# Neighbourhood attention: one biased pass over a unit's own and context scores, one exponential per unit

## The chip, the cores and the metric

The kernel runs on one core of a Trainium2 chip. The metric is the device time of one execution in microseconds (us); lower is better. The kernel before took 2827.46 us as the median of 3 runs (2826.29 to 2831.8).

## The reference

Two layers work on 1024 latent tokens (a grid of 16 rows by 64 columns, 1024 features) and 256 context tokens. Each layer projects the tokens, mixes them in four head groups A to D, projects the result, and then routes tokens through 16 experts. The change is in group A, 2-D neighbourhood attention with 4 heads of 64 features. A query attends to the 8 x 16 latent keys around it, with a learned bias by offset, and, without bias, to all 256 context keys; one softmax runs over both:

```python
s_win = (einsum('bqhd,brqjhd->bhqrj', q_row, k_win) * scale + bias).reshape(B, H, GRID_W, nw)
s_ctx = einsum('bqhd,blhd->bhql', q_row, kc) * scale
p = softmax(concatenate([s_win, s_ctx], axis=-1), axis=-1)
out = einsum('bhqrj,brqjhd->bqhd', p_win, v_win) + einsum('bhql,blhd->bqhd', p_ctx, vc)
```

## The kernel before

**Units.** `mixers` (L2047) makes a list of units and hands it to `pipeline` (L722). In group A a unit is 128 queries (two grid rows) of one head: 8 units to a head, 32 to a layer, numbered here 0 to 31. A head's units 0, 1, 6 and 7 are outer ones: they score 8 rows of keys (512 columns). Units 2 to 5 are inner ones (9 rows, 576 columns). In layer 0 four context units run ahead of group A; after it, in both layers, come the units of group D. Two units that follow each other (`q` 0 and 1) are a pair and share the tiles `pth` and `ptl`, the sums and the output `oA`.

**A unit's steps.** `scores` (L849): PE multiplies queries with keys into two PSUM tiles `SA`, the first with 256 or 320 columns, the second with 256 columns of own keys and 256 of the context. The DVE pass `window` (L858; on the chip one CUSTOM instruction and one that reads its accumulator) adds the bias table `tt`, keeps the maximum and writes to the SBUF tile `P` (PA in the trace). Own columns go through it in two passes; the context's 256 have only their maximum taken (L872). L874 takes the maximum over the three: `nmA`, negated. `exps` (L877): ACT takes the exponential of the context part out of PSUM (L883), then of the own part within `P` (L886), each with its sum. In an inner unit POOL sets a pad of 64 columns in `P` to 0 (L882). `turn` (L889): PE transposes 128-column chunks of `P` into PSUM tiles `pT`, up to four chunks to a tile, ACT copies each to `pth` (L104, rounded), and DVE writes the rest to `ptl` (L105): first the 2 context chunks, then 4, then (inner) 1. `values` (L903): PE multiplies them with the values into `oA`; ACT copies that to `oT` (L699), PE turns it back into `oP`, and ACT scales it by the reciprocal of the summed sums (`inv_sums`, L702) into `oh` (L717).

**Order.** On PE, DVE and ACT the order of instructions is the order in which `pipeline` writes them; each engine runs its list in order. Stage s interleaves, in rounds, the scores of unit s + 1, the exponentials of unit s and the turn of unit s - 1: a round runs each of the three up to its next `yield`. After the rounds comes one step of side work and then `values` and `finish` of earlier units. `oT` is written in even stages; the first half of a pair's products with the values, and `oP` and `oh` of the pair before, in odd ones. Side work of prep_d (L1050), a tile `hT4` (PE transposes, an ACT copy, a DVE rest) per stage, lies in stages 15 to 22 of both layers and 28 to 31 of layer 0. POOL's list is made by a scheduler.

**Buffers.** PSUM tiles `SA` take 4 banks (`m1`); `pT`, `hT4`, `oA` and `oP` share 4 more (`b1`, L94), a new tile taking the one that has been given back longest.

```python
                todo = []
                if s + 1 < n:
                    todo.append(units[s + 1].scores())
                if 0 <= s < n:
                    todo.append(units[s].exps())
                if 1 <= s <= n:
                    todo.append(units[s - 1].turn())
```

Of the kernel before, what the change touches and what calls it, by code (L numbers as in the profile page):

```python
# [13 lines left out]
AF = mybir.ActivationFunctionType  # L14
ALU = mybir.AluOpType
AX = mybir.AxisListType
# [15 lines left out]
NEG = -1e30  # L32
# [15 lines left out]
def f32(ap):  # L48
    return ap.bitcast(F32)
# [27 lines left out]
class Kernel:  # L77
# [730 lines left out]

    def bias_tables(self, i, h):

        nc, a = self.nc, self.a
        raw = self.half([128, 16, 64], name="tabr")
        nc.gpsimd.memset(raw, 0.0)
        pad = a["na_pad"]
        src = bass.AP(tensor=pad.tensor, offset=pad.offset + (i * H + h) * 15 * 128, ap=[[1, 64], [128, 15], [1, 64]])

        nc.sync.dma_start(raw[0:64, 0:15], src)
        nc.sync.dma_start(raw[64:128, 1:16], src)
        for _ in range(4):
            yield  # L820
        tt = self.wpage([128, 23, 64], name="tt")
        m = self.cmask[:, None, :].to_broadcast([128, 14, 64])
        nc.gpsimd.tensor_tensor(tt[:, 0:14], raw[:, 1:15, ::-1], m, ALU.add)
        nc.gpsimd.tensor_copy(tt[:, 14:23], tt[:, 2:11])
        nc.gpsimd.memset(tt[64:128, 14], NEG)
        nc.gpsimd.memset(tt[0:64, 22], NEG)
        self.tabs[h] = tt
        yield

    def units_a(self, i, out):  # L830
        nc, k = self.nc, self

        class Unit:
            delays = ()

            def __init__(u, h, g, q, first):
                u.h, u.g, u.q = h, g, q
                u.first = first or u
                u.inner = g in (1, 2)
                u.r = 4 * g + 2 * q  # L840
                u.k0 = min(max(u.r - 4, 0), 8)
                u.nk = 9 if u.inner else 8
                u.w = u.nk * 64
                u.n = 5 if u.inner else 4
                u.c_lo = (0, 0, 2, 4)[g]

            def scores(u):
                q = k.qA[u.h][:, u.r * 64:u.r * 64 + 128]

                w, k0 = u.w - 256, u.k0 * 64  # L850
                u.S = k.m1([128, 512], name="SA"), k.m1([128, 512], name="SA")
                k_h, tt = k.kA[u.h], k.tabs[u.h]
                u.P = k.half([128, 6 * 128 + 256], name="PA")
                mx = k.small([128, 3], name="mxA")
                s0 = 14 if u.inner else u.k0 - u.r + 6
                bias = tt[:, s0:s0 + u.nk].rearrange("p s k -> p (s k)")

                def window(j, S, c):  # L858
                    nc.vector.tensor_tensor_reduce(out=u.P[:, c], in0=S, in1=bias[:, c], op0=ALU.add, op1=ALU.max,
                                                   scale=1.0, scalar=-3e38, accum_out=mx[:, j:j + 1])  # L860

                def dot(S, keys):
                    k.mm(S, q, keys[0], True, False)
                    k.mm(S, q, keys[1], False, True)

                dot(u.S[0][:, :w], [x[:, k0:k0 + w] for x in k_h])
                window(0, u.S[0][:, :w], slice(0, w))
                yield
                dot(u.S[1][:, :256], [x[:, k0 + w:k0 + w + 256] for x in k_h])
                dot(u.S[1][:, 256:], k.kAc[u.h])  # L870
                window(1, u.S[1][:, :256], slice(w, w + 256))
                nc.vector.tensor_reduce(mx[:, 2:3], u.S[1][:, 256:], axis=AX.X, op=ALU.max)  # L872
                u.nm = k.small([128, 1], name="nmA")
                nc.vector.tensor_reduce(u.nm, mx, axis=AX.X, op=ALU.max, negate=True)  # L874
                yield

            def exps(u):  # L877
                if u.q == 0:
                    u.sums = k.small([128, 2, 2], name="smA")
                w, P, sm = u.w, u.P, u.first.sums[:, u.q]  # L880
                if u.inner:
                    nc.gpsimd.memset(P[:, w:w + 64], 0.0)  # L882
                nc.scalar.activation(P[:, u.n * 128:u.n * 128 + 256], u.S[1][:, 256:], AF.Exp, bias=u.nm,  # L883
                                     accum_out=sm[:, 1:2])
                yield
                nc.scalar.activation(P[:, :w], P[:, :w], AF.Exp, bias=u.nm, accum_out=sm[:, 0:1])  # L886
                yield

            def turn(u):  # L889
                if u.q == 0:  # L890
                    u.pth, u.ptl = k.wpage([128, 8, 256], F32R, name="pth"), k.wpage([128, 8, 256], F32R, name="ptl")

                c0 = u.k0 // 2 - u.c_lo
                qq = slice(u.q * 128, (u.q + 1) * 128)
                pth, ptl = u.first.pth, u.first.ptl
                if u.inner:
                    z = 5 if u.q == 0 else 0
                    nc.gpsimd.memset(f32(pth[:, z, qq]), 0.0)
                    nc.gpsimd.memset(f32(ptl[:, z, qq]), 0.0)
                yield from k.pt_steps(pth[:, 6:8, qq], ptl[:, 6:8, qq], u.P[:, u.n * 128:], 2)  # L900
                yield from k.pt_steps(pth[:, c0:c0 + u.n, qq], ptl[:, c0:c0 + u.n, qq], u.P, u.n)

            def values(u, part):  # L903
                ch = [(c, k.vA[(u.c_lo + c) // 2][:, (u.c_lo + c) % 2, u.h]) for c in range(6 if u.inner else 4)]
                ch += [(6 + c, k.vA[4][:, c, u.h]) for c in range(2)]
                n = len(ch) // 2
                if part == 0:
                    u.o2 = k.b1([128, 256], name="oA")
                    u.rs = k.inv_sums(u.sums)
                for j in range(part * n, part * n + n):  # L910
                    c, v = ch[j]
                    k.pv1(u.o2, v, u.pth[:, c], u.ptl[:, c], j == 0, j == len(ch) - 1)
                if part:
                    u.oT = k.heads_T(u.o2)

            def after(u, step):
                if u.q == 0 and step in (3, 4):
                    u.values(step - 3)
                if u.q == 0 and step == 5:
                    u.finish()  # L920

            def finish(u):
                k.put_heads(u.oT, u.rs, lambda q: out(u.h, 2 * u.g + q), lambda: u.done(u.h, 2 * u.g + 1))

        units = []
        for h in range(H):
            for g in range(4):
                for q in range(2):
                    units.append(Unit(h, g, q, units[-1] if q else None))
        return units  # L930
# [1292 lines left out]
```

## Time and profile before

| what | us |
|---|---|
| median of 3 runs | 2827.46 |
| the profiled execution | 2829.49 |
| its span, first to last instruction | 2827.7 |
| PE busy in the span | 2684.8 (95%) |
| DVE busy | 2088.3 (74%) |
| ACT busy | 1710.8 (61%) |
| POOL busy | 339.6 (12%) |
| group A, layer 0, 329.5 to 422.8 | 93.3 |
| group A, layer 1, 1822.0 to 1909.5 | 87.5 |

The busy shares of the whole span are means over stages that have little in common. Group A is 6% of the span, so it has to be read by itself: by the busy time in its own two stretches, and by the rows of its own instructions. Matmuls are pipelined and overlap in the trace, so that a PE shown as busy may still be waiting a little between them.

### The profile page before, as it was taken

How to read it: one execution, taken by the hardware profiler on the slowest of the kernel's cores; microseconds unless marked ns; L12 is line 12 of the kernel's file. 1: busy time of each engine (PE TensorE's matmuls, PEld its weight loads, DVE VectorE, ACT ScalarE, POOL GpSimd, SP SyncE). 2: the span in 40 equal slices, each digit the busy share in tenths (PEclk: the TensorE clock that was granted, in tenths of full speed). 3: DMA queues.
4: the chain of work that ended last, by engine and by line, in shares of the span. 5: the costliest groups of instructions: out<-in, count | busy, mean ns of one | idle time of the engine just before them, and what ended most of it. 6: DMA issues, size and time to landing. Idle time of an engine off the chain costs nothing. (4 is left out here: it accounts for less than half of the span.)

```text
span 2827.7 us, 46563 instructions
## 1 busy us (share of the span) xinstructions
PE 2684.8 (95%) x17078; PEld 2129.7 (75%) x17078; DVE 2088.3 (74%) x4377; ACT 1710.8 (61%) x3319; POOL 339.6 (12%) x418
## 2 busy tenths in 40 slices
PE   7999899999899999999999999999999699999995
PEld 5788788887577777777765788788876588888874
DVE  5624687867887777777765842698868998999996
ACT  5522697965455555555544641597963577777774
POOL 0000120211111110101111001120211000010011
PEclk9999999999999999999999999999999799999998
DMA  7652311144978888888899555111154799999996
GB/s 306 211 149 63 78 34 49 61 150 173 325 266 286 285 289 285 302 287 291 294 342 340 166 198 149 42 42 49 57 174 163 282 368 359 380 388 385 384 378 243
DMA packets 234572, 641.37 MB, mean 227 GB/s; under 512 B 35654, under 2 KB 90566, under 8 KB 234344
## 3 DMA queue, kind: packets, MB, share of 16 engines
q1 hardware_dynamic: 212264, 590.61, 56.9%
q0 software_dynamic: 21936, 47.72, 6.9%
q8 instruction: 135, 2.21, 0.3%
q14 instruction: 93, 0.76, 0.1%
q10 hardware_dynamic: 144, 0.07, 0.0%
HBM read 576.80 MB, written 61.54 MB: 226 GB/s over the span
## 5 line engine op out<-in xcount | busy, mean ns | idle before, releaser
L104 ACT ACTIVATE ewh<-ewr 128x1024 fp32r<-128x1024 f32 x768 | 772.9, 1055 | 425.5 <-DMA ewr<-exp_w_up 145.4
L105 DVE TENSOR_TENSOR ewl<-ewr,ewh 128x1024 fp32r<-128x1024 f32 x768 | 894.0, 1218 | 152.7 <-ACT ewh L104 150.8
L111 PE MATMUL moeP<-ewh,xs 128*128 128x512 f32 x2048 | 665.5, 400 | 3.6 <-DVE xs L105 3.4
L111 PEld LDWEIGHTS moeP<-ewh,xs 128*128 128x128 f32 x2048 | 385.9, 189 | 102.7 <-issue 10.5
L111 PE MATMUL moeP<-ewl,xs 128*128 128x512 f32 x1024 | 407.4, 398 | 0.0
L111 PE MATMUL moeP<-ewh,ehs 128*128 128x512 f32 x1024 | 331.3, 397 | 1.3 <-DVE ehs L105 1.3
L111 PEld LDWEIGHTS moeP<-ewh,ehs 128*128 128x128 f32 x1024 | 192.2, 188 | 56.4 <-issue 10.3
L111 PEld LDWEIGHTS moeP<-ewl,xs 128*128 128x128 f32 x1024 | 194.0, 189 | 43.9 <-issue 2.3
L111 PE MATMUL mixp<-woh,cT 128*128 128x512 f32 x576 | 205.1, 410 | 0.0
L111 PE MATMUL moeP<-ewl,ehs 128*128 128x512 f32 x512 | 201.7, 394 | 0.1
L1606 PE MATMUL cx<-ewr,cxo 128*32 128x256 f32 x3072 | 189.3, 382 | 0.8 <-DVE cxo L1835 0.8
L105 DVE TENSOR_TENSOR ptl<-pT,pth 128x512 fp32r<-128x512 f32 (+2 forms) x288 | 164.3, 580 | 19.6 <-ACT pth L104 18.8
L120 PE MATMUL pT<-ident,PA 128*128 128x128 f32 x928 | 146.0, 275 | 8.3 <-ACT oh L717 3.7
L1606 PEld LDWEIGHTS cx<-ewr,cxo 128*32 128x32 f32 x3072 | 90.9, 110 | 82.8 <-issue 30.3
L104 ACT ACTIVATE pth<-pT 128x512 fp32r<-128x512 f32 (+2 forms) x288 | 149.5, 536 | 4.3 <-PE pT L120 1.3
L1106 DVE TENSOR_REDUCE mxA<-SD 128x1 f32<-128x512 f32 (+1 forms) x192 | 114.5, 597 | 38.4 <-PE SD L111 37.5
L120 PEld LDWEIGHTS pT<-ident,PA 128*128 128x128 f32 x928 | 112.7, 141 | 32.4 <-ACT oh L717 5.8
L111 PEld LDWEIGHTS mixp<-woh,cT 128*128 128x128 f32 x576 | 108.3, 188 | 24.9 <-issue 3.8
L111 PE MATMUL SD<-kT,qT 96*128 96x512 f32 x384 | 119.8, 420 | 5.8 <-ACT PA L1120 5.4
L111 PE MATMUL mixp<-wol,cT 128*128 128x512 f32 x288 | 113.4, 394 | 0.0
L111 PEld LDWEIGHTS moeP<-ewl,ehs 128*128 128x128 f32 x512 | 96.3, 188 | 22.3 <-DVE ewl L105 1.0
L1565 POOL DMA_INDIRECT xg<-hrow,tkii x32 | 55.8, 1743 | 416.4 <-PE tkp L111 95.2
(425 smaller groups left out, 5143.5 us busy)
## 6 DMA issues: line engine op xcount, KB each, us to landing
ewr<-exp_w_gate SPq DMA_DIRECT2D x132, 1024.0 KB
ewr<-exp_w_up SPq DMA_DIRECT2D x132, 1024.0 KB
ewr<-exp_w_down SPq DMA_DIRECT2D x132, 1024.0 KB
ada_w<-ada_w SPq DMA_DIRECT2D x96, 512.0 KB
qkv<-qkvr SPq DMA_DIRECT2D x18, 512.0 KB
xacc<-xm SPq DMA_DIRECT2D x18, 512.0 KB
hrow<-xm SPq DMA_DIRECT2D x18, 512.0 KB
fr<-w_in SPq DMA_DIRECT2D x16, 512.0 KB
```

Of the source, the lines that this page charges most:

```text
L104: self.nc.scalar.activation(hi, src, AF.Copy)
L105: self.parted = (lo_on or self.nc.vector).tensor_tensor(lo, src, f32(hi), ALU.subtract)
L111: self.nc.tensor.matmul(out, l, r, start=start, stop=stop)
L120: self.nc.tensor.transpose(out, src, self.ident[:p, :p])
L1106: nc.vector.tensor_reduce(mx[:, j:j + 1], u.S[j], axis=AX.X, op=ALU.max)
L1565: nc.gpsimd.indirect_dma_start(out=xg, out_offset=None, in_=self.hrow[0], in_offset=bass.IndirectOffsetOnAxis(ap=idl, axis=0))
L1606: nc.tensor.matmul(pc[32 * j:32 * j + 32, :], xc[:, k % 2, k // 2], raw[:, j * 256:(j + 1) * 256], start=(k == 0), stop=(k == KT - 1), til ...
```

## The change

- The bias table gets 4 more rows of 64 columns, set to 0 by POOL. The second pass of `window` runs over all 512 columns of the second `SA` tile at once: 256 own ones with their bias, 256 of the context with the zeros, written to two ranges of `P` (`ranges`). The separate maximum over the context falls away.
- One exponential within `P` over 768 (outer) or 896 columns (inner, the pad included) takes the place of two. The pad is set to -1e30 ahead of it, in `scores`, and no longer to 0 in `exps`. One sum per unit is left, so the addition of sums (L704) falls away.
- `turn` begins with the first 4 chunks. Where the own chunks end at place 6 (units 3 and 5 of a head) the 5 + 2 chunks are turned as 4 and 3; otherwise own chunks (4, or 4 and 1) come first and the context's 2 last.
- `exps` has one `yield` in place of two.

```diff
-        tt = self.wpage([128, 23, 64], name="tt")
+        tt = self.wpage([128, 27, 64], name="tt")
+        nc.gpsimd.memset(tt[:, 23:27], 0.0)
...
+    def ranges(self, x, c0, step):
+
+        x = x[:, c0:c0 + 256]
+        return bass.AP(tensor=x.tensor, offset=x.offset, ap=[x.ap[0], [step, 2], [1, 256]])
...
-                mx = k.small([128, 3], name="mxA")
+                if u.inner:
+                    nc.gpsimd.memset(P[:, u.w:u.w + 64], NEG)
+                mx = k.small([128, 2], name="mxA")
...
-                window(1, u.S[1][:, :256], slice(w, w + 256))
-                nc.vector.tensor_reduce(mx[:, 2:3], u.S[1][:, 256:], axis=AX.X, op=ALU.max)
+                window(1, u.S[1].rearrange("p (a k) -> p a k", a=2), k.ranges(P, w, gap),
+                       k.ranges(bias, b1, 23 * 64 - b1))
...
-                if u.inner:
-                    nc.gpsimd.memset(P[:, w:w + 64], 0.0)
-                nc.scalar.activation(P[:, u.n * 128:u.n * 128 + 256], u.S[1][:, 256:], AF.Exp, bias=u.nm,
-                                     accum_out=sm[:, 1:2])
-                yield
-                nc.scalar.activation(P[:, :w], P[:, :w], AF.Exp, bias=u.nm, accum_out=sm[:, 0:1])
+                P = u.P[:, :u.n * 128 + 256]
+                nc.scalar.activation(P, P, AF.Exp, bias=u.nm, accum_out=u.first.sums[:, u.q:u.q + 1])
                 yield
...
-                yield from k.pt_steps(pth[:, 6:8, qq], ptl[:, 6:8, qq], u.P[:, u.n * 128:], 2)
-                yield from k.pt_steps(pth[:, c0:c0 + u.n, qq], ptl[:, c0:c0 + u.n, qq], u.P, u.n)
+                if c0 + u.n == 6:
+                    yield from k.pt_steps(pth[:, c0:8, qq], ptl[:, c0:8, qq], u.P, u.n + 2)
+                else:
+                    yield from k.pt_steps(pth[:, c0:c0 + u.n, qq], ptl[:, c0:c0 + u.n, qq], u.P, u.n)
+                    yield from k.pt_steps(pth[:, 6:8, qq], ptl[:, 6:8, qq], u.P[:, u.n * 128:], 2)
...
-                    u.rs = k.inv_sums(u.sums)
+                    u.rs = k.small([128, 2], name="rr")
+                    nc.vector.reciprocal(u.rs, u.sums)
```

ACT in stage 5 of layer 0, from the exponential of unit 5 to that of unit 6 (the `pT` and `pth` are those of unit 4; names carry their numbers), before:

```order
L883 ACTIVATE PA_3553,smA_3558<-SA_3552,nmA_3574 128x256
L104 ACTIVATE pth_3605<-pT_3609 128x2x128
L886 ACTIVATE PA_3553,smA_3558<-PA_3553,nmA_3574 128x576
L104 ACTIVATE pth_3605<-pT_3623 128x4x128
L104 ACTIVATE pth_3605<-pT_3630 128x128
L717 ACTIVATE oh_3649<-oP_3646,rr_3542 128x64 x2
L883 ACTIVATE PA_3598,smA_3659<-SA_3597,nmA_3620 128x256
```

and with the change:

```order
L892 ACTIVATE PA_3546,smA_3552<-PA_3546,nmA_3568 128x896
L104 ACTIVATE pth_3592<-pT_3596 128x4x128
L104 ACTIVATE pth_3592<-pT_3610 128x128
L104 ACTIVATE pth_3592<-pT_3614 128x2x128
L717 ACTIVATE oh_3633<-oP_3630,rr_3536 128x64 x2
L892 ACTIVATE PA_3586,smA_3643<-PA_3586,nmA_3608 128x768
```

What the chunks of unit 4 wait behind has moved: before, two chunks followed a short exponential; now the four chunks come first, behind the long one.

DVE in the same stage, from the first pass of unit 6 (PA_3598 before, PA_3586 now; the second row of a pass reads its accumulator) to the end of unit 4's rests, before:

```order
L859 ISA PA_3598,mxA_3599<-SA_3596,tt_3250 128x256
L859 ISA mxA_3599 128x1
L105 TENSOR_TENSOR ptl_3606<-pT_3609,pth_3605 128x2x128
L859 ISA PA_3598,mxA_3599<-SA_3597,tt_3250 128x256
L859 ISA mxA_3599 128x1
L872 TENSOR_REDUCE mxA_3599<-SA_3597 128x1
L874 TENSOR_REDUCE nmA_3620<-mxA_3599 128x1
L105 TENSOR_TENSOR ptl_3606<-pT_3623,pth_3605 128x4x128
L105 TENSOR_TENSOR ptl_3606<-pT_3630,pth_3605 128x128
```

and with the change:

```order
L870 ISA PA_3586,mxA_3587<-SA_3584,tt_3250 128x256
L870 ISA mxA_3587 128x1
L105 TENSOR_TENSOR ptl_3593<-pT_3596,pth_3592 128x4x128
L870 ISA PA_3586,mxA_3587<-SA_3585,tt_3250 128x512
L870 ISA mxA_3587 128x1
L885 TENSOR_REDUCE nmA_3608<-mxA_3587 128x1
L105 TENSOR_TENSOR ptl_3593<-pT_3610,pth_3592 128x128
L105 TENSOR_TENSOR ptl_3593<-pT_3614,pth_3592 128x2x128
```

The rest of the four chunks has moved from behind the unit's maximum `nmA` to ahead of it.

PE in stage 19 of layer 0, an odd stage with an inner unit's turn and side work, from the turn of unit 18 (`PA_4198` before, `PA_4147` now) to the first product of the pair before with the values; the tiles of `b1` are taken in this order, and `oP` is the next of them, six rows on. Before:

```order
L120 MATMUL pT_4309<-ident_75,PA_4198 128x128 x2
L111 MATMUL SA_4297<-kAh_3071,qA_2824 128x256
L111 MATMUL SA_4297<-kAl_3072,qA_2824 128x256
L111 MATMUL SA_4297<-kAc_3116,qA_2824 128x256 x2
L120 MATMUL pT_4323<-ident_75,PA_4198 128x128 x4
L120 MATMUL pT_4330<-ident_75,PA_4198 128x128
L120 MATMUL hT4_4338<-ident_75,tokp_4021 96x128 x4
L111 MATMUL oA_4345<-pth_4204,vA_1890 128x256
```

and with the change:

```order
L120 MATMUL pT_4255<-ident_75,PA_4147 128x128 x4
L111 MATMUL SA_4243<-kAh_3071,qA_2824 128x256
L111 MATMUL SA_4243<-kAl_3072,qA_2824 128x256
L111 MATMUL SA_4243<-kAc_3116,qA_2824 128x256 x2
L120 MATMUL pT_4269<-ident_75,PA_4147 128x128
L120 MATMUL pT_4273<-ident_75,PA_4147 128x128 x2
L120 MATMUL hT4_4282<-ident_75,tokp_3981 96x128 x4
L111 MATMUL oA_4289<-pth_4154,vA_1890 128x256
```

The three `pT` held 2, 4 and 1 chunks in this order; now they hold 4, 1 and 2, so that the four chunks lie one place further back from `oA` and `oP`.

## Rows read from the trace of the kernel before

**Rows 1.** Windows, group A of both layers: length, busy us (count) by engine, PEclk, DMA, GB/s

```profile
329.50:422.80 93.30, 87.04 (x705) 81.41 (x704) 83.29 (x318) 85.82 (x280) 20.67 (x60) 1.00 0.21 57
1822.00:1909.50 87.50, 82.67 (x655) 78.15 (x656) 79.22 (x304) 81.49 (x259) 20.66 (x60) 0.97 0.15 38
```

**Rows 2.** Tile SA, layer 0 then layer 1: ns min/median/max, first to last start

```profile
L883 ACT ACTIVATE PA<-SA,nmA x32: 467/476/635, 333.1 to 422.8; 128x256 f32<-128x256 f32 x32
...
L883 ACT ACTIVATE PA<-SA,nmA x32: 467/474/634, 1823.3 to 1909.5; 128x256 f32<-128x256 f32 x32
```

**Rows 3.** Waits, 329.5 to 422.8: waiter <- releaser: us in total, times, longest

```profile
ACT oh L717 <- PE oP L111: 4.4, 9, 1.1
```

**Rows 4.** Timeline of ACT, stage 10 of layer 0: start, us, instruction [idle before]

```profile
359.14 0.48 ACT L883 ACTIVATE PA<-SA,nmA 128x256 f32<-128x256 f32 x1
...
359.59 0.39 ACT L104 ACTIVATE pth<-pT 128x256 fp32r<-128x256 f32 x1
359.85 0.79 ACT L886 ACTIVATE PA<-PA,nmA 128x576 f32<-128x576 f32 x1
...
360.61 0.61 ACT L104 ACTIVATE pth<-pT 128x512 fp32r<-128x512 f32 x1
...
361.35 0.51 ACT L883 ACTIVATE PA<-SA,nmA 128x256 f32<-128x256 f32 x1
```

**Rows 5.** Timeline of ACT, stage 0 of layer 0, where a context unit turns

```profile
333.13 0.47 ACT L883 ACTIVATE PA<-SA,nmA 128x256 f32<-128x256 f32 x1 [0.85 <-DVE nmA L874]
...
333.60 0.59 ACT L104 ACTIVATE pch<-pT 128x512 fp32r<-128x512 f32 x1
334.08 0.72 ACT L886 ACTIVATE PA<-PA,nmA 128x512 f32<-128x512 f32 x1
...
334.78 0.38 ACT L699 ACTIVATE oT<-oA 128x256 f32<-128x256 f32 x1
...
335.81 0.47 ACT L883 ACTIVATE PA<-SA,nmA 128x256 f32<-128x256 f32 x1 [0.24 <-DVE nmA L874]
```

**Rows 6.** Timeline of DVE, the same stage

```profile
334.22 0.69 DVE L105 TENSOR_TENSOR pcl<-pT,pch 128x512 fp32r<-128x512 f32 x1 [0.53 <-ACT pch L104]
334.82 0.41 DVE L859 CUSTOM_DVE_ANT_0 PA<-SA,tt 128x256 f32<-128x256 f32 x1
335.16 0.08 DVE L859 DVE_READ_ACCUMULATOR2_ANT mxA<- 128x1 f32 x1
335.16 0.42 DVE L872 TENSOR_REDUCE mxA<-SA 128x1 f32<-128x256 f32 x1
335.62 0.16 DVE L874 TENSOR_REDUCE nmA<-mxA 128x1 f32<-128x3 f32 x1
```

**Rows 7.** Groups by form, 329.5 to 422.8: busy us, mean ns | idle before

```profile
L859 DVE CUSTOM_DVE_ANT_0 PA<-SA,tt 128x256 f32<-128x256 f32 x48 | 19.8, 413 | 0.4 <-PE SA L111 0.4
...
L859 DVE CUSTOM_DVE_ANT_0 PA<-SA,tt 128x320 f32<-128x320 f32 x16 | 7.6, 477 | 0.0
...
L104 ACT ACTIVATE pth<-pT 128x128 fp32r<-128x128 f32 x16 | 5.0, 312 | 0.0
...
L105 DVE TENSOR_TENSOR ptl<-pT,pth 128x128 fp32r<-128x128 f32 x16 | 4.5, 280 | 0.0
```

**Rows 8.** Timeline of all engines, stage 19 of layer 0

```profile
384.02 0.47 ACT L883 ACTIVATE PA<-SA,nmA 128x256 f32<-128x256 f32 x1
...
386.13 0.89 DVE L105 TENSOR_TENSOR ptl<-pT,pth 128x512 fp32r<-128x512 f32 x2
...
386.87 0.66 PE L111 MATMUL oP<-ident,oT 128*128 128x64 f32 x4 [0.49 <-DVE ptl L105]
...
387.57 0.52 ACT L717 ACTIVATE oh<-oP,rr 128x64 f32<-128x64 f32 x2 [0.84 <-PE oP L111]
...
387.98 0.47 ACT L883 ACTIVATE PA<-SA,nmA 128x256 f32<-128x256 f32 x1
```

**Rows 9.** Timeline of POOL, stage 9 of layer 0

```profile
359.04 0.15 POOL L882 MEMSET PA<- 128x64 f32 x1
```

More of the change, by code (lines that the diff above doesn't have):

```diff
@@ L852, in scores, with window @@
                 k_h, tt = k.kA[u.h], k.tabs[u.h]
-                u.P = k.half([128, 6 * 128 + 256], name="PA")
-                mx = k.small([128, 3], name="mxA")
+                u.P = P = k.half([128, 6 * 128 + 256], name="PA")
+                if u.inner:
+                    nc.gpsimd.memset(P[:, u.w:u.w + 64], NEG)
+                mx = k.small([128, 2], name="mxA")
                 s0 = 14 if u.inner else u.k0 - u.r + 6
-                bias = tt[:, s0:s0 + u.nk].rearrange("p s k -> p (s k)")
-                def window(j, S, c):
-                    nc.vector.tensor_tensor_reduce(out=u.P[:, c], in0=S, in1=bias[:, c], op0=ALU.add, op1=ALU.max,
+                bias = tt.rearrange("p s k -> p (s k)")
+                b1, gap = s0 * 64 + w, u.n * 128 - w
+                def window(j, S, out, bias):
+                    nc.vector.tensor_tensor_reduce(out=out, in0=S, in1=bias, op0=ALU.add, op1=ALU.max,
                                                    scale=1.0, scalar=-3e38, accum_out=mx[:, j:j + 1])
@@ L866, in scores @@
                 dot(u.S[0][:, :w], [x[:, k0:k0 + w] for x in k_h])
-                window(0, u.S[0][:, :w], slice(0, w))
+                window(0, u.S[0][:, :w], P[:, :w], bias[:, s0 * 64:b1])
                 yield
@@ L878, in exps @@
                 if u.q == 0:
-                    u.sums = k.small([128, 2, 2], name="smA")
-                w, P, sm = u.w, u.P, u.first.sums[:, u.q]
-                if u.inner:
-                    nc.gpsimd.memset(P[:, w:w + 64], 0.0)
-                nc.scalar.activation(P[:, u.n * 128:u.n * 128 + 256], u.S[1][:, 256:], AF.Exp, bias=u.nm,
-                                     accum_out=sm[:, 1:2])
-                yield
-                nc.scalar.activation(P[:, :w], P[:, :w], AF.Exp, bias=u.nm, accum_out=sm[:, 0:1])
+                    u.sums = k.small([128, 2], name="smA")
+                P = u.P[:, :u.n * 128 + 256]
+                nc.scalar.activation(P, P, AF.Exp, bias=u.nm, accum_out=u.first.sums[:, u.q:u.q + 1])
                 yield
```

## The prediction

> **What bounds group A now.** All that changes lies in group A, so I read the windows of its two stretches first [rows 1]: 93.3 and 87.5 us, with PE, DVE and ACT each busy for 89 to 94% of them. No engine can be named from that; ACT's idle time is 7.5 of 93.3 us, and the largest entry of it is `oh` waiting for `oP` [rows 3]. The tile view gives the pace: 32 context exponentials from 333.1 to 422.8, and from 1823.3 to 1909.5 [rows 2]: 31 stages in 89.7 and 86.2 us, 2.9 and 2.8 us each. ACT's timeline shows what an undisturbed stage is [rows 4]: exponential, copy, exponential, copy, `oT`, next exponential, back to back, 2.21 us, nothing waited for. So ACT's own work (more of it where there is side work) sets the pace, and removing work from ACT looks like a gain.
>
> That holds only while ACT never waits for `nmA`. One stage of the trace shows what happens when it does. In stage 0 of layer 0 the unit that turns is a context unit, whose four chunks are copied at once, right behind an exponential. There ACT stands still 0.24 us for DVE's `nmA` [rows 5], and DVE 0.53 us for ACT's copy [rows 6]. The two engines run in a ring: exponential 333.13, copy 333.60, rest 334.22, pass 334.82, maximum 335.16, `nmA` 335.62, next exponential 335.81: 2.68 us, with both engines idle in it. A ring cannot go faster than the sum of its links, however much work is taken off either engine.
>
> **The change, part by part.** The order on ACT and DVE shows that the change makes this ring the rule: the four chunks of unit s - 1 are copied right behind unit s's one exponential, and their rest now stands ahead of the second pass and `nmA` of unit s + 1, for which the next exponential waits. Before, only two chunks stood in the ring (exponential to copy 0.45, [rows 4]); the long exponential and the four chunks lay outside. The links now:
>
> - Exponential to copy. 512 columns take 0.70 us (334.08 to 334.78, [rows 5]), 576 take 0.76 (359.85 to 360.61, [rows 4]); 0.06 per 64 more columns gives 0.94 for 768 and 1.06 for 896. With the rounding of the rows (0.05 to 0.07 per 64): 0.90 to 0.98 and 1.00 to 1.12.
> - Copy of 512 to its rest: 333.60 to 334.22, 0.62.
> - Rest of 512 to the pass: 334.22 to 334.82, 0.60.
> - The pass over 512: 256 columns hold DVE for 0.34 (334.82 to 335.16, [rows 6]); 64 more cost 477 - 413 = 64 ns [rows 7], so 256 more cost 0.26: 0.60. Writing to two ranges is in no row; I take nothing for it, at most 0.05.
> - Its accumulator is read in 0.08, and a dependent instruction starts 0.04 after the end of the one before (335.16 + 0.42 to 335.62): 0.12.
> - `nmA` to the exponential: 335.62 to 335.81, 0.19.
>
> Sum: 3.07 us in a stage whose exponential is an outer unit's, 3.19 in an inner one's. No stage can be shorter. ACT's own work falls below it in nearly all of them, so 3.1 takes the place of 2.2 to 3.0.
>
> Layer 0's 31 intervals hold 16 inner and 15 outer ones: 16 x 3.19 + 15 x 3.07 = 97.1 against 89.7: +7.4. In layer 1 nothing is turned in stage 0, which costs the exponential alone: 0.94 + 16 x 3.19 + 14 x 3.07 = 95.0 against 86.2: +8.8.
>
> **The buffers.** `oP` takes the bank of the fourth `b1` tile before it. In stage 19 this was the four-chunk `pT`: DVE took up its rest at 386.13, PE began `oP` at 386.87, 0.05 us after the end of that rest (0.69 long), ACT began `oh` 0.70 later, and the next exponential came 0.41 after that [rows 8]. With the change the four chunks come first, so the fourth tile before `oP` is another one:
>
> - Odd stages with an inner turn and no side work (3, 5, 11, 13, 27; in layer 1 also 29): now the four-chunk `pT`, before the two-chunk one. Exponential 1.06, copy 0.62, rest 0.69, then 0.05 + 0.70 + 0.41: 3.53, or 0.34 more than the ring. 5 and 6 stages: 1.7 and 2.0.
> - The same with side work (19, 21, 29; in layer 1 only 19, 21): now the one-chunk `pT`, whose rest stands behind `nmA`. 1.06 + 0.62 + 0.60 + 0.60 + 0.12 to `nmA`, 0.07 more until DVE takes the rest up (an instruction starts 0.09 before the end of one that lasts 0.16, as at 334.82), 0.28 for it [rows 7], and 0.05 + 0.70 + 0.41: 4.51, against 3.96 in stage 19 before (384.02 to 387.98) and 1.32 more than the ring. 3 and 2 stages: 4.0 and 2.6.
> - Odd outer ones with side work (15, 17): the four-chunk `pT`; 0.94 + 0.62 + 0.69 + 1.16 = 3.41, 0.34 more. 2 and 2 stages: 0.7 and 0.7.
>
> Together +6.4 and +5.3. What could spare them: a bank that comes free earlier than I think; the low end is nothing.
>
> **What is taken away is paid in slack.** Per unit, ACT loses 0.45 + 0.70 or 0.76 and gains 0.94 or 1.06; per layer DVE loses 32 context maxima, 16 additions of sums and 8 rests, ACT 8 copies. None of this is in the ring except the context maximum, which is in its sum already. POOL gets eight zero fills of the table's new rows, and the pads are set in `scores`. The exponential now waits for the pad; before, unit 11's was set at 359.04 [rows 9] and its exponential began at 361.35 [rows 4], 2.3 us later, so I take nothing. If POOL were late, ACT's whole queue would stand behind the exponential. PE's matmuls are the same in number; the second `SA` tile is given back by DVE's pass, earlier than by an exponential. No DMA is added; the stores of `oh` only come later, and nothing waits for them in group A. What follows (group D, projection, experts) runs behind it on the same engines and starts as much later.
>
> **Sum.** 7.4 + 8.8 + 6.4 + 5.3 = 27.9. The profiled execution took 2829.49 us (span 2827.7), 2.0 over the median of 2827.46; so 2857.4 against the former and **2855** against the latter. Differences under about 0.2% (5.7 us) could not be told from none.
>
> **Rivals.**
>
> *Faster: the work counts, not the ring.* If `nmA` always came before ACT had ended its own list, ACT's saving would be the gain: per layer 32 x 0.18 (0.21 outer, 0.15 inner) plus 8 copies at some 0.2 (0.31 for one of 128 columns, [rows 7], less what the wider one takes more), 7.4 us, so -15 and 2813. For it: ACT is the busiest engine by its timeline. It decides if the ring falls under ACT's remaining work, 2.45 us per stage ((85.82 - 7.4) / 32, [rows 1]); with the links as read it would have to lose over 0.6 us, and stage 0 shows them at full length. The Trainium skill, Perfetto Trace Analysis, Optimizing Scalar/DVE Operations, says that grouping into larger operations can improve throughput if the engine is saturated, which would give this rival's time; the same section says that breaking instructions up may let work be completed sooner where engines cause bubbles. By rows 5 and 6 it is the second that applies here.
>
> *Slower, but by the ring alone.* If the banks cost nothing, 16.2 remains: 2844. For it: banks are given out by age, and I follow them by counting.
>
> *No change.* The lost time could be made up by something later that waits anyway. Against it: DMA is 0.21 and 0.15 busy in these windows [rows 1], so nothing runs ahead in them. 2827.
>
> *Slower by PE's clock.* The granted clock is 1.00 and 0.97 [rows 1]; with PE waiting in each stage it could fall to the lower level (1.2 of 2.4 GHz). PE is busy 87.04 us for 32 units, 2.7 each; doubled it is 5.4 in place of 3.1. Six such stages would add 14: 2869.
>
> **Chances and range.** The forecast 0.70, the ring alone 0.13, the work rival 0.07, no change 0.04, the clock 0.06. So faster 0.07, same 0.04, slower 0.89. The links' bounds are worth 0.05 us a stage, 3 us; the range takes in the ring alone and the clock: 2842 to 2870.
>
> **What would show it.** In the profile after: exponential to exponential 3.07 in outer stages and 3.19 in inner ones with no side work, never under 3; ACT waiting for `nmA` in most stages, some 0.5 us each, in place of hardly ever; DVE waiting for the four-chunk copy in each stage; group A's windows near 107 and 102 us; `oh` waiting for `oP` in the odd inner stages, longest in stages 19, 21 and 29; PE's work, and all after group A, as before. I am wrong on the ring if exponentials follow each other under 2.8 us, on the buffers if stage 19 takes under 4 us, and on the rest if the loss lies outside group A.

## The result, and the profile after

The changed kernel took 2862.44 us (median of 4 runs, 2860.13 to 2868.03) against 2828.97 (median of 4) for the kernel before on the same chip: ratio 1.0115, 95% interval 1.0101 to 1.0129, slower by 33 us. Forecast were 2855 and +27.9. The profiled execution took 2861.94, its span is 2860.2, 32.5 longer than before.

Windows of group A in the two layers and of the 277 us behind it, after (columns as in [rows 1], with the busy time and count of PE, of its weight loads, of DVE, ACT and POOL in this order):

```profile
331.50:439.20 107.70, 91.28 (x711) 82.19 (x711) 77.87 (x264) 81.13 (x211) 21.14 (x62) 1.00 0.18 49
1839.30:1943.00 103.70, 87.92 (x652) 79.42 (x653) 74.28 (x251) 75.71 (x189) 22.09 (x65) 0.95 0.12 32
439.20:716.40 277.20, 266.97 (x1793) 226.43 (x1791) 208.02 (x550) 206.11 (x612) 38.52 (x38) 1.00 0.31 107
```

ACT and DVE do less than before (81.13 and 77.87 us against 85.82 and 83.29 in layer 0, [rows 1]), in a longer time: the work went down and the idle time up. What follows is untouched: 277.2 us of the kernel before (422.8 to 700.0) held 267.34 us of PE and 206.96 of DVE.

The one exponential that is left, by its line, in each layer (count, ns min/median/max, first to last start), to be held against [rows 2]:

```profile
L892 ACT ACTIVATE PA<-PA,nmA x32: 933/992/1047, 335.1 to 439.2; 128x768 f32<-128x768 f32 x16, 128x896 f32<-128x896 f32 x16
...
L892 ACT ACTIVATE PA<-PA,nmA x32: 932/988/1047, 1840.6 to 1943.0; 128x768 f32<-128x768 f32 x16, 128x896 f32<-128x896 f32 x16
```

31 stages in 104.0 and 102.4 us, where it was 89.7 and 86.2: +14.3 and +16.2, so 30.5 of the 32.5 lie in group A. The other 2.0 are there before it: the first exponential starts at 335.15 in place of 333.13. Between the two layers' stages 1.0 more is lost, and behind the second 1.0 is won. I do not put the 2.0 down to the change: in the profiles of the runs below, whose code ahead of group A is the same, the first exponential starts anywhere from 331.1 to 335.3.

Waits between 329.5 and 440 (waiter <- releaser: us, times, longest):

```profile
DVE ptl L105 <- ACT pth L104: 25.3, 29, 1.2
...
ACT oh L717 <- PE oP L111: 10.8, 10, 1.8
ACT PA L892 <- DVE nmA L885: 10.1, 18, 1.2
PEld oP L111 <- DVE ptl L105: 6.3, 7, 1.4
```

DVE waits 29 times for ACT's copy, ACT 18 times for DVE's `nmA`, and `oh` waits 10.8 us for `oP` where it was 4.4 [rows 3].

Stage 0 of layer 0, ACT and then DVE (start, us, instruction [idle before]), to be held against [rows 5, 6]:

```profile
335.15 0.94 ACT L892 ACTIVATE PA<-PA,nmA 128x768 f32<-128x768 f32 x1 [0.78 <-DVE nmA L885]
...
336.08 0.57 ACT L104 ACTIVATE pch<-pT 128x512 fp32r<-128x512 f32 x1
...
338.21 0.94 ACT L892 ACTIVATE PA<-PA,nmA 128x768 f32<-128x768 f32 x1 [0.87 <-DVE nmA L885]
```

```profile
336.69 0.69 DVE L105 TENSOR_TENSOR pcl<-pT,pch 128x512 fp32r<-128x512 f32 x1 [0.99 <-ACT pch L104]
337.30 0.68 DVE L870 CUSTOM_DVE_ANT_1 PA<-SA,tt 128x512 f32<-128x512 f32 x1
337.90 0.08 DVE L870 DVE_READ_ACCUMULATOR2_ANT mxA<- 128x1 f32 x1
338.02 0.15 DVE L885 TENSOR_REDUCE nmA<-mxA 128x1 f32<-128x2 f32 x1
```

This is the ring, link by link: 0.93 to the copy, 0.61 to the rest, 0.61 to the pass, 0.60 to its accumulator, 0.12 to `nmA`, 0.19 to the next exponential, 3.06 us. ACT stands still 0.87 of them and DVE 0.99.

Stage 5 of layer 0, all engines, an odd stage with an inner turn:

```profile
351.03 1.04 ACT L892 ACTIVATE PA<-PA,nmA 128x896 f32<-128x896 f32 x1 [0.95 <-POOL PA L862]
...
352.07 1.01 ACT L104 ACTIVATE pth<-pT 128x512 fp32r<-128x512 f32 x3
...
352.68 0.69 DVE L105 TENSOR_TENSOR ptl<-pT,pth 128x512 fp32r<-128x512 f32 x1 [0.93 <-ACT pth L104]
353.42 0.66 PE L111 MATMUL oP<-ident,oT 128*128 128x64 f32 x4 [0.71 <-DVE ptl L105]
...
354.12 0.52 ACT L717 ACTIVATE oh<-oP,rr 128x64 f32<-128x64 f32 x2 [1.04 <-PE oP L111]
354.53 0.93 ACT L892 ACTIVATE PA<-PA,nmA 128x768 f32<-128x768 f32 x1
```

PE begins `oP` 0.05 us after the end of the four-chunk rest, ACT's `oh` follows, the next exponential stands behind it: 3.50 us. (The POOL of the first row is the fill of the pad, which ended 0.18 us before that exponential; `nmA` had started 0.24 before, as it does ahead of the other inner ones, so the pad did not hold it longer than them.) Stages 19, 21 and 29 take 4.49 each.

### The profile page after: what moved, and what is told of

It reads as the page before. It is cut to its first block, busy times and chain, and to the rows that moved or that the text cites. A ratio compares the mean times of both kernels' runs of the same rounds, so it can differ in the third digit from the quotient of the medians.

```text
span 2860.2 us, 46327 instructions
## 1 busy us (share of the span) xinstructions
PE 2693.7 (94%) x17078; PEld 2129.6 (74%) x17078; DVE 2079.0 (73%) x4265; ACT 1700.6 (59%) x3175; POOL 340.0 (12%) x426
## 5 line engine op out<-in xcount | busy, mean ns | idle before, releaser
L111 PE MATMUL moeP<-ewh,ehs 128*128 128x512 f32 x1024 | 331.1, 397 | 1.3 <-DVE ehs L105 1.3
L111 PEld LDWEIGHTS moeP<-ewh,ehs 128*128 128x128 f32 x1024 | 192.1, 188 | 56.7 <-issue 10.3
L105 DVE TENSOR_TENSOR ptl<-pT,pth 128x512 fp32r<-128x512 f32 (+3 forms) x272 | 163.0, 605 | 60.1 <-ACT pth L104 57.9
L104 ACT ACTIVATE pth<-pT 128x512 fp32r<-128x512 f32 (+3 forms) x272 | 139.8, 539 | 4.8 <-PE pT L120 2.4
```

Of the source, the lines that this page charges most:

```text
L104: self.nc.scalar.activation(hi, src, AF.Copy)
L105: self.parted = (lo_on or self.nc.vector).tensor_tensor(lo, src, f32(hi), ALU.subtract)
L111: self.nc.tensor.matmul(out, l, r, start=start, stop=stop)
```

## The experiments

Ratios are to the kernel before on the same chip. The last two columns are the 31 stages of group A in us, first to last exponential, in the profile of each; they hold none of the scatter outside.

| run | ratio, interval | layer 0 | layer 1 |
|---|---|---|---|
| before | 1 | 89.7 | 86.2 |
| the change | 1.0115 [1.0101, 1.0129] | 104.0 | 102.4 |
| e1 rests late | 1.0009 [1.0000, 1.0019] | 90.5 | 89.0 |
| e2 two chunks first | 1.0036 [1.0024, 1.0049] | 95.7 | 91.3 |
| e3 before, four first | 1.0018 [1.0008, 1.0028] | 92.4 | 91.1 |
| e4 `oP` ahead of the values | 1.0120 [1.0103, 1.0137] | 109.4 | 104.8 |
| e5 a reduce in the ring | 1.0137 [1.0121, 1.0152] | 109.8 | 107.3 |
| e6 the same outside it | 1.0111 [1.0095, 1.0126] | 105.9 | 102.1 |
| e7 `oP` in a score tile | 1.0076 [1.0062, 1.0090] | 102.1 | 99.4 |
| e8 = e1 + e7 | 0.9976 [0.9966, 0.9985] | 86.3 | 83.7 |
| e9 = e8 + two first | 0.9977 [0.9966, 0.9988] | 87.8 | 84.4 |
| e10 before + e7 | 0.9976 [0.9968, 0.9985] | 86.0 | 82.4 |
| e11 before + e1 + e7 | 1.0008 [0.9999, 1.0017] | 91.8 | 86.7 |
| e12 = e8 + `oA` in a score tile | 1.0005 [0.9996, 1.0014] | 90.2 | 89.8 |

**e1: the rests behind `nmA`.** One number in `units_a` of the change makes the pipeline issue the split of a turned tile (ACT's copy and DVE's rest) one round later, behind the second pass and `nmA`:

```
-            delays = ()
+            delays = (0,)
```

> The change, with the copies of a group A unit's chunks and their rests written one round later, so that on DVE the rest of the four chunks stands behind nmA of the next unit; the work of every engine is the same. Ring theory: nmA no longer waits for the exponential of the stage, the ring is gone, and only ACT's work (2.45 us a stage) and oP's waits for its bank (3.5 us in odd inner stages, 4.2 in stages 19, 21 and 29) remain: about 89 us from the first to the last exponential of layer 0 against 104 with the change, so 30 to 36 us less than the change, 2826 to 2834, near the kernel before. ACT's wait for nmA falls from 10 us in layer 0 to under 2. Rival (the wider passes or the longer exponential themselves cost the time): within 5 us of the change.

1.0009: nearly the whole loss is gone, though ACT and DVE run as many instructions as in the change (3175 and 4265). Waits of this run, 329.5 to 426:

```profile
ACT oh L717 <- PE oP L111: 13.0, 11, 2.1
...
ACT PA L892 <- DVE nmA L885: 0.8, 1, 0.8
...
DVE ptl L105 <- ACT pth L104: 0.8, 2, 0.4
```

The ring's two waits went from 25.3 and 10.1 to 0.8 each, and stages of 1.94 to 2.3 us appear, which the ring forbade. The bank's wait grew instead: later rests free it later, and stages 19 and 21 take 4.75 and 4.70.

**e2: the context's two chunks turned first**, as before the change.

```
-                if c0 + u.n == 6:
-                    yield from k.pt_steps(pth[:, c0:8, qq], ptl[:, c0:8, qq], u.P, u.n + 2)
...
+                yield from k.pt_steps(pth[:, 6:8, qq], ptl[:, 6:8, qq], u.P[:, u.n * 128:], 2)
+                yield from k.pt_steps(pth[:, c0:c0 + u.n, qq], ptl[:, c0:c0 + u.n, qq], u.P, u.n)
```

> The change, with the chunks turned in the order of before: the context's 2 first, then 4, then 1. Ring theory: two chunks stand in the ring in place of four: 0.94 or 1.06 + 0.41 + 0.36 + 0.60 + 0.12 + 0.19 = 2.62 in outer and 2.74 in inner stages, with oP's banks as before; stages 19, 21 and 29 near 3.9. Some 88 us per layer: 2820 to 2832, 30 to 42 less than the change. No stage with side work apart, the exponentials follow each other by 2.62 to 2.75, hardly ever less. Rival (the merged exponential costs the time): within 5 us of the change.

The plain stages came out as worked out, 2.64 and 2.75: a copy and a rest of two chunks make shorter links. The total did not, 22 us under the change where 30 to 42 were expected: stages 19, 21 and 29 of layer 0 take 4.41, and the even ones beside them (20, 22, 28, 30) 3.4 to 3.7. PE and ACT in stage 19 of this run (387.11 to 391.52):

```profile
389.02 0.39 PE L111 MATMUL oA<-pth,vA 128*128 128x256 f32 x1 [0.27 <-DVE ptl L105]
...
390.42 0.66 PE L111 MATMUL oP<-ident,oT 128*128 128x64 f32 x4 [0.41 <-DVE ptl L105]
...
391.11 0.52 ACT L717 ACTIVATE oh<-oP,rr 128x64 f32<-128x64 f32 x2 [1.48 <-PE oP L111]
```

`oA` and `oP` both wait for rests, and every copy ahead of those now stands behind one exponential of 1.04 us, where the two-chunk copy stood behind one of 0.47. I had moved only the ring.

**e3: the kernel before, with the four chunks first.** The reverse edit of e2, in the kernel before.

> The kernel before, with the turn order of the change alone (first 4 chunks; 4 and 3 where they fit), two exponentials and two passes kept. Ring theory: the ring is 0.45 + 0.62 + 0.60 + 0.34 + 0.46 + 0.19 = 2.66, under most of the stages of before, and oP's wait costs little: 2824 to 2836, within 8 us of before. Rival (the order of the chunks alone costs the time, through the banks): 10 to 30 us slower than before.

1.0018, and 2.68 us in the plain stages. The order of the turns alone costs a sixth of the loss: the four-chunk copy behind a *short* exponential is a ring that ACT's own work nearly fills. With e2 the four corners are there: the new order alone costs 0.18%, the merged pass and exponential in the old order 0.36%, both together 1.15%. It takes the long exponential and the order together.

**e4: `oP` and `oh` ahead of the values in odd stages**, to spare `oP` the late bank.

```
...
+                if u.q == 0 and step == 3:
+                    if u.prev:
+                        u.prev.finish()
+                    u.values(0)
...
```

> The change, with oP and oh of the pair before written ahead of the first products with the values in odd stages, so that oP takes a bank that comes free a stage earlier. Bank theory: odd inner stages without side work 3.5 to 3.2, stages 19, 21 and 29 from 4.5 to some 3.6, odd outer ones with side work 3.4 to 3.1: 8.5 us less than the change in the two layers together, 2850 to 2857; the ring stays. Rival (these stages are long for another reason than oP's bank): within 2 us of the change.

A miss that teaches. Odd inner stages fell to 3.22 to 3.24 and stages 19 and 21 to 3.50 as the bank theory says, but even stages of 4.1 to 6.2 appeared and the sum got worse. PE in stages 5 and 6, then their windows (columns as in [rows 1]):

```profile
351.60 0.55 PE L111 MATMUL oA<-pth,vA 128*128 128x256 f32 x1 [1.39 <-DVE ptl L105]
...
353.87 1.05 PE L120 MATMUL pT<-ident,PA 128*128 128x128 f32 x4
```

```profile
349.10:352.34 3.24, 1.40 (x7) 1.29 (x8) 2.27 (x8) 2.47 (x7) 0.00 (x0) 0.88 0.68 126
352.34:357.12 4.78, 4.78 (x33) 4.78 (x32) 2.43 (x10) 2.44 (x6) 0.00 (x0) 0.72 0.25 45
```

The wait passed from `oP` to `oA`, which takes the late bank now: PE stands still 1.39 us. Then eight matmuls of the values stand ahead of the next scores and transposes, and in the stage behind the gap the granted clock is 0.72, part of it at the lower level: four transposes take 1.05 us, where the same four in the changed kernel (at 357.15) take 0.60. The clock is not all of it: stage 20 takes 4.12 with 1.00 granted.

**e5 and e6: one more reduce, in the ring and outside it.** The context's maximum once more, 256 columns, read by nobody:

```
 # e5
+                nc.vector.tensor_reduce(k.small([128, 1], name="mxB"), u.S[1][:, 256:], axis=AX.X, op=ALU.max)
                 nc.vector.tensor_reduce(u.nm, mx, axis=AX.X, op=ALU.max, negate=True)
 # e6
                 nc.vector.tensor_reduce(u.nm, mx, axis=AX.X, op=ALU.max, negate=True)
+                nc.vector.tensor_reduce(k.small([128, 1], name="mxB"), u.S[1][:, 256:], axis=AX.X, op=ALU.max)
```

> The change plus one more VectorE reduce in every unit of group A: the maximum of the context's 256 score columns once more, into a tile that nobody reads, placed right AHEAD of the reduce nmA. It is 0.35 to 0.45 us of VectorE by itself. Ring theory (the prediction's): it lies on the ring second pass -> nmA -> exponential -> copy -> rest, so every stage grows by its price: plain outer stages 3.06/3.13 -> 3.5 to 3.6, plain inner 3.23 -> 3.65, about +22 to +28 us over the change, ratio to the kernel before 1.019 to 1.022. Rival, VectorE has room (75 us busy of 104 in group A of a layer) and what counts is the work of the busiest engine, PE: +0 to +3 us, ratio 1.011 to 1.0125, the same for this run and for the next.

> The same extra reduce in every unit, placed right BEHIND nmA, so the same work, but not between a rest and the next nmA that waits for it. Ring theory: it falls into the 1.5 us in which VectorE waits for the next 4-chunk copy anyway; plain stages stay at 3.06 to 3.23, at most the stages that wait for a bank (whose rests come behind it) grow: 0 to +5 us over the change, ratio 1.011 to 1.0135. A theory by VectorE's work gives this run the same time as the one with the reduce ahead of nmA.

DVE in stage 2 of e5, layer 0:

```profile
336.82 0.68 DVE L870 CUSTOM_DVE_ANT_0 PA<-SA,tt 128x512 f32<-128x512 f32 x1
337.43 0.08 DVE L870 DVE_READ_ACCUMULATOR2_ANT mxA<- 128x1 f32 x1
337.43 0.42 DVE L885 TENSOR_REDUCE mxB<-SA 128x1 f32<-128x256 f32 x1
337.77 0.14 DVE L886 TENSOR_REDUCE nmA<-mxA 128x1 f32<-128x2 f32 x1
```

Ahead of `nmA` every ring stage grows by the same amount, 3.06 to 3.27, 3.13 to 3.34, 3.23 to 3.44. Behind it the same work leaves them at 3.06, 3.13 and 3.23. So it is place, not work, that costs. The size was expected too large: the reduce lasts 0.42, but begins together with the read of the accumulator, and puts `nmA` back by 0.22 (0.34 behind 337.43, where it was 0.12 behind 337.90). The stages that wait for a bank answer as their chains say: those of 3.50, whose chain has no `nmA` in it, stay at 3.50 in e5 and e6, but for two of e5 (3.79 and 3.59) that were granted a clock of 0.85 and 0.89; stages 19 and 21, whose chain has, go from 4.49 to 4.70 in e5, and to 4.83 in e6, where the reduce stands ahead of the rest that frees the bank.

**e7: `oP` in a score tile.** Columns 384 to 511 of the first score tile of a unit are never written, and DVE has read the rest of it by then; `oP` goes there and takes no `b1` bank:

```
...
+                p = None
+                if u.at + 6 < len(units):
+                    p = units[u.at + 6].S[0][:, 384:512].rearrange("p (q d) -> p q d", q=2)
...
```

> The change with the output transposes oP written into the unused columns 384 to 511 of a score tile that the vector engine has already read, so oP takes no bank of the 4-bank ring b1 and waits for no rest of the transposed chunks; nothing is reordered. Bank theory (the prediction's second term): the waits of the copies oh for oP (10.8 us in group A of the first layer) go, odd inner stages 3.50 -> 3.23, stages 19, 21, 29 4.49 -> 3.3 to 3.9; sum 6 to 10 us less than the change, ratio 1.0080 to 1.0095. Stages without these waits stay at 3.06 to 3.23, since the ring is untouched. Rival, the waits for oP are only another face of the ring (the same time would be waited for elsewhere): no gain, 1.0115 as the change.

The odd inner stages without side work fall to the ring, 3.50 to 3.23, and so do the odd outer ones with some in layer 0, 3.39 to 3.07 and 3.46 to 3.19. Stages 19, 21 and 29 were expected at 3.3 to 3.9 and hardly move: 4.21, 4.52 and 4.44, where they took 4.49. Waits of this run, 329.5 to 438, and PE in stage 19:

```profile
ACT PA L892 <- DVE nmA L885: 18.2, 26, 1.2
...
PE oA L111 <- DVE ptl L105: 6.7, 9, 1.2
...
ACT oh L717 <- PE SA L111: 4.5, 3, 1.7
```

```profile
398.00 0.38 PE L111 MATMUL oA<-pth,vA 128*128 128x256 f32 x1 [1.14 <-DVE ptl L105]
```

`oh` now waits three times and not ten, ACT for `nmA` 26 times and not 18: what the banks had covered belongs to the ring. In the three stages it is `oA` that waits, because, by counting, the side work's `hT` takes one more bank of the four.

**e8: both cures in the change.**

> Both cures at once: rests of the turned chunks behind nmA (run 1 of the first set) and oP in the score tiles. If ring and banks are two separate causes that add up, the first cure left odd stages of 3.6 to 4.9 us by the banks, and these should fall to 2.3 to 3.0: group A 82 to 87 us in a layer against 90.5 and 89.0 with the rests late alone, 7 to 12 us less, ratio to the kernel before 0.9965 to 0.9985. If after the ring the group is bound by PE's work (88 us busy of 104 in a layer's group A after the change, so at least about 85 us), it ends at the upper end of that. Rival: the odd stages wait for something else, and the run is at 1.001 as with the rests late alone.

0.9976, where e1 alone gave 1.0009 and e7 alone 1.0076: the two causes are separate, and without both the changed kernel is faster than before by 0.24%. The odd inner stages without side work (5, 11, 13, 27) take 2.77 to 2.94, where they took 3.6 in e1. Stage 19 of this run, ACT, DVE and PE:

```profile
382.91 1.06 ACT L892 ACTIVATE PA<-PA,nmA 128x896 f32<-128x896 f32 x1
...
387.23 0.52 ACT L717 ACTIVATE oh<-SA,rr 128x64 f32<-128x64 f32 x2 [1.58 <-PE SA L111]
387.64 1.04 ACT L892 ACTIVATE PA<-PA,nmA 128x896 f32<-128x896 f32 x1
```

```profile
385.05 1.21 DVE L105 TENSOR_TENSOR ptl<-pT,pth 128x512 fp32r<-128x512 f32 x3
```

```profile
385.87 0.36 PE L111 MATMUL oA<-pth,vA 128*128 128x256 f32 x1 [0.91 <-DVE ptl L105]
```

4.73 us: the first of the three rests, 0.69 long, ends at 385.74, and `oA` gets its bank.

**e9, e10, e11: what the change itself is worth.** e9 is e8 with the turns of e2, e10 the kernel before with the edit of e7 alone, e11 the kernel before with those of e1 and e7.

> The change with the context's two chunks turned first again (2, 4, 1), the rests behind nmA, and oP in the score tiles. With neither ring nor oP's bank left, the order of the turns should matter little: the 2-chunk copy and its rest come earlier, but there is one more tile in the 4-bank ring b1 in odd inner units. Same as the run with 4 and 3 (0.9976) within 0.0015 if rings are what counted; 3 to 8 us longer (0.9985 to 1.0005) if the number of b1 tiles is what is left.

> The kernel before (two exponentials, turns 2, 4, 1) with only oP in the score tiles. Bank theory: the copies oh waited 4.4 us for oP in group A of the first layer, so at most about 4 us a layer go: -2 to -8 us, ratio 0.997 to 0.9993. If the single pass and exponential of the change are worth nothing by themselves, this kernel is as fast as the change with both cures (0.9976).

> The kernel before with both cures: rests behind nmA, oP in the score tiles. In the kernel before the ring runs over the short 256-column exponential and the 2-chunk rest, and gives stages of 2.25 to 2.9 us; putting the rests behind nmA frees it only partly. If fewer instructions were worth something once ring and banks are gone, this run is slower than the change with both cures (0.9976) by 2 us or more, at 0.9985 to 1.001; if not, it is equal or faster, 0.995 to 0.9976.

e10 is as fast as e8 and e9, with the two exponentials and all the small instructions that the change takes away. So the new home of `oP` alone gives the kernel before all that e8 gained. e11 is slower than e8, as I had expected of a kernel to which fewer instructions are worth something; e10 shows another cause beside it. The late rests cost e11 0.32% against e10: stages 19 and 21 take 4.18 and 4.22, against 3.27 and 3.48 in e10. In layer 0 they cost 0.6 to 0.9 us in each of the stages 19 to 22 and 28 to 30, 0.7 in stage 5 and 0.4 in stage 13, and in the others 0.1 or less; in stages 0 and 3 they win 0.4 and 0.2.

Windows of group A, first to last exponential of layer 0, of e8, and then of e10:

```profile
335.05:421.37 86.32, 80.91 (x674) 77.75 (x673) 75.17 (x254) 75.67 (x201) 21.28 (x62) 1.00 0.23 61
```

```profile
333.30:419.30 86.00, 81.59 (x673) 77.94 (x673) 79.67 (x308) 82.28 (x271) 20.64 (x60) 1.00 0.23 62
```

ACT does 6.6 us less in e8, and the time is the same. But it is not spent in the same stages. In stages 19, 21 and 29 e8 loses 4.1 us to e10 (4.73, 4.70 and 5.00 against 3.27, 3.48 and 3.62), where by the rows above `oA` waits for a late rest; the other 28 stages of layer 0 are 3.7 us shorter together, stages 24 to 27 by 0.18 to 0.24 each in both layers. So the merging does save time in some stages, about what the prediction had ACT save (0.15 to 0.21), and e8 gives it back elsewhere. Whether rests late only in the stages without side work would keep it, no run shows. PE has the same work in both and is busy 94% and 95%; no run takes work off PE, so whether it is the next bound stays open.

**e12: `oA` too in a score tile**, the second one of a unit, to free stages 19, 21 and 29.

```
...
-                    u.o2 = k.b1([128, 256], name="oA")
+                    t = u.at + 4
+                    u.o2 = units[t].S[1][:, :256] if t < len(units) else k.b1([128, 256], name="oA")
...
```

> The change with the rests behind nmA, oP in the free columns of a score tile, and the values' products oA in the other score tile of a unit (its scores have been read by the second biased pass, which only the change makes possible: before, the exponential still read them). Where the run with both cures still has stages of 4.7 to 5.0 us (19, 21, 29 of the first layer: oA waits for the rest that frees its bank, oh waits behind it), these should fall to 3.0 to 3.5, and the stages around 2.3 to 3.0 stay. Four such stages and a fifth in the two layers: 5 x 1.3 to 1.7 = 6 to 9 us less than the change with both cures (0.9976), ratio 0.9943 to 0.9962, faster than both kernels. Rival: oA in the score tile makes the next score matmul wait for oT, or PE's own work is the bound, and the time stays at 0.997 to 0.999.

The three stages fell to 3.66, 3.88 and 3.79 from 4.73, 4.70 and 5.00, as hoped, but most other odd stages rose from between 2.65 and 3.06 to between 3.55 and 3.74: 1.0005, a miss, slower even than the rival's 0.997 to 0.999. Its waits, 329.5 to 421.5:

```profile
ACT oh L717 <- PE SA L111: 12.9, 12, 1.5
...
PE SA L111 <- DVE mxA L870: 5.0, 9, 0.7
```

`oA` no longer waits for a rest, but for the second pass to have read the tile's scores, and ACT's queue again stands behind `oh`.

## Why the prediction was right, step by step

| term | forecast | measured |
|---|---|---|
| ring, outer and inner stage | 3.07, 3.19 | 3.06 or 3.13, 3.23 |
| ring, both layers | 16.2 | 19.5 |
| bank, inner without side work | 3.53 | 3.50 |
| bank, 19, 21, 29 | 4.51 | 4.49 |
| bank, outer 15 and 17 | 3.41 | 3.39, 3.46; in layer 1 3.39, 3.83 |
| banks, both layers | 11.7 | 10.3 |
| PE's clock | 0 | 0.7 |
| before group A | 0 | 2.0 |
| sum | 27.9 | 32.5 |

The banks' measured sum is each bank stage's excess over the ring (0.27 for 3.50, 1.26 for 4.49 and so on); the ring's is what is left of 30.5. That the sum came so near is luck in part: the ring was forecast 3.3 too low and the banks 1.4 too high, and 2.0 lie outside the mechanism.

*The ring* held link by link and was undersized by 3.3 us, 0.05 a stage. The largest part is the last link: ahead of an inner unit's exponential and of some outer ones it is 0.25 us, not 0.19. ACT and DVE, end of stage 4 of the changed kernel:

```profile
347.55 0.15 DVE L885 TENSOR_REDUCE nmA<-mxA 128x1 f32<-128x2 f32 x1
...
347.80 1.04 ACT L892 ACTIVATE PA<-PA,nmA 128x896 f32<-128x896 f32 x1 [1.18 <-DVE nmA L885]
```

33 of the 62 stages end with it, which makes 2.0 of the 3.3. The waits in the trace tell the two apart (the views leave semaphore instructions out). In 31 of these 33 a separate semaphore instruction on ACT's queue waits for `nmA`, and the exponential itself waits for something else: in the inner ones for POOL's pad, which I had taken for nothing because the pad is early, in the outer ones (9, 15, 17, 25 and 31 in layer 0) for earlier work of ACT. In the 12 units whose exponential itself waits for `nmA`, with nothing else in its way, the link is 0.19, also in units 7 and 23 of layer 0, which have a second wait. Outer unit 9 takes 0.25 with the separate instruction, and 0.18 in e5, where it has none. So the 0.06 goes with this instruction and not with the pad.

*The banks* held too, all but stage 3 of both layers, which was to take 3.53 and took 3.23 and 3.24. I had miscounted there: the first pair's `oP` comes in stage 5 (at 353.42 in layer 0), and stage 3 has none, so 0.7 of the forecast 11.7 was for nothing. e7 shows that the waits for `oP` are these 3.50 and 3.39; of the 4.49 only a small part was `oP`'s alone, since without it `oA` waits nearly as long. Why stage 17 takes 3.83 in layer 1 stays open; e7 takes 3.56 there and 3.19 in layer 0.

*The work rival* (0.07) is out: no stage but the first of layer 1, where nothing is turned, is under 3.06, and the time went up. (By [rows 1] the busiest engine was PE, with 87.04 us, and not ACT, as this rival had it.) The saving is not worthless for all that: against e10 it shows in stages 24 to 27 of e8. The sentence of the Trainium skill, Perfetto Trace Analysis, Optimizing Scalar/DVE Operations, on breaking instructions up where engines that are not saturated cause bubbles is what the trace agrees with: in the change ACT and DVE are busy for 75% and 72% of group A's window of layer 0, and with the exponential and the pass in two pieces and the same turns (e3) the plain stages take 2.68 us and not 3.06 to 3.23.

*PE's clock* (0.06) lengthened one stage, stage 12 of layer 1 (3.97 us, 0.62 granted), after PE had stood 1.12 us for a rest. (Stages 0 and 1 of layer 1 run at the lower level too, 0.50, but so they do in the kernel before.) PE there, and one stage later:

```profile
1877.60 1.11 PE L120 MATMUL pT<-ident,PA 128*128 128x128 f32 x4
...
1881.17 0.60 PE L120 MATMUL pT<-ident,PA 128*128 128x128 f32 x4
```

It cost 0.7 us once and not 2.3 six times; e4, where PE had stood 1.39 us and the stage behind took 4.78 at 0.72, and stage 12 of layer 0 in e6, 4.15 at 0.59, show that it can count.

*No change* and *the ring alone* are out by the interval and by the 3.50 and 4.49.

## What to carry to other kernels

Ahead of merging instructions on an engine that looks busy, write down which instruction of each engine the other waits for in its own order, and sum the links: a merged instruction ends later for whoever waits for its first part, and two queues that wait for each other once a stage cannot go faster than that sum, whatever work is removed. The cure is a place, not a price: moving the rests behind `nmA` gave back 1.06 of the 1.15%, with every instruction kept. It is a cure for a ring that binds: in the kernel before, with `oP` in a score tile, the same move cost 0.32% (e11 against e10). And when a bank of a small ring is the wait, give the tile another home that is free by then, instead of reordering around it: reordering handed the wait to the next tile (e4), the unused columns of a score tile did not (e7, e10), and a tile still being read did (e12).

## What the runs showed of the hardware that I had not expected

- A reduce of 0.42 us placed between a pass with an accumulator and the instruction that needs it costs 0.22, not 0.42: it starts together with the accumulator's read, 0.12 before `nmA` otherwise would, and `nmA` starts 0.08 before its end (e5).
- An exponential starts 0.19 us behind the start of `nmA` where it waits for `nmA` itself, and 0.25 where a separate semaphore instruction ahead of it does, whatever its own other wait is for and however long that had been over (the changed kernel; unit 9 of layer 0 0.25, and 0.18 in e5).
- Behind a PE that had stood 1.12 and 1.39 us (stage 12 of layer 1; e4, stage 6) came a stretch at the lower clock level, in stages that took 0.7 and 1.7 us more than the ring; in the second the order of PE's work has its part. In stage 1 of layer 0 of the changed kernel PE stood 1.45 us (until 340.32) and nothing of the kind followed.
